# Weights, remainders, activations and 4 KB tiles at four offsets within 2048 bytes of a partition

## The chip, the cores and the metric

One core of a Trainium2 chip runs the kernel. The metric is the device time of one execution in microseconds. The kernel before was timed in three runs; one more execution was profiled, and all rows below come from that one.

## The reference, cut to what matters

Two transformer-like blocks are applied to one sequence of 256 tokens with 2048 features, all in float32.

```python
def reference(x, ...):
    x = first_block(x, ...)    # conv branch + forgetting attention, gated, then relu^2 MLP (d_ff 8192)
    return second_block(x, c, ...)   # ada-modulated: MoBA attention + SSM mixer, then conv FFN (5632 x 2)
```

Nearly all of the work is products of the 256 x 2048 activations with large weight matrices (`w_in`, `w_ff1`, `w_ff2`, `w_up`, `w_down` and smaller ones), 434 pieces of 1 MB in this kernel, and one vector-matrix product, `silu(c) @ w_ada`, of 96 MB.

## The kernel before, in words

**High and low parts.** The matmul engine takes `float32r` operands, which are rounded. To keep the accuracy of float32, each operand is kept as a high part (the value converted to `float32r`) and a remainder (the value less its high part), and three products are summed: high x high, high x remainder, remainder x high.

**Pieces.** A weight matrix is packed on the host into pieces of 128 partitions x 2048 columns (8 KB per partition). `piece` (line 102) takes one: the SP queue loads it to `wraw` (line 62), the scalar engine copies it to `wH` with a conversion (line 122), the vector engine subtracts `wH` from `wraw` and writes the remainder `wL` (line 123). `wraw`, `wH` and `wL` have three buffers each in the pool `wp`. A piece is converted at once or, where it is waited for, in four parts of 512 columns.

```python
raw = wp.tile([P, 2048], F32, tag="wraw", ...)                      # 106
h = wp.tile([P, 2048], FR, tag="wH", ...)                           # 108
l = wp.tile([P, 2048], FR, tag="wL", ...)                           # 109
...
A.activation(h[:, sl], raw[:, sl], AF.Copy)                         # 122
ins = V.tensor_tensor(l[:, sl], raw[:, sl], h[:, sl].bitcast(F32), op=OP.subtract)   # 123
```

**Two kinds of product.** `bblock` (line 139) and `wide` (line 186) give a transposed result: the piece is the stationary operand, the activations move. One piece is 16 matmuls with 128 x 128 blocks of `wH` over 512 columns (the high part and the remainder of an activation chunk side by side) and 16 with blocks of `wL` over 256 columns (the high part alone). These are the projections `cc`, `cv`, `cb`, `gc`, `ga`, `q`, `k`, `z`, `co`, `ao`, `ff1` and `up`. `ablock` (line 229) and `down_last` (line 955) give a result with tokens on the partitions: the activations are stationary, the piece moves. One piece is 24 matmuls of 512 columns: `uh` with `wH`, `ul` with `wH`, `uh` with `wL`. These are `v`, `mix`, `wo`, `ff2` and `dn`. Every matmul has a weight load of its own, and all go through `mm` (line 128).

```python
def hi(k, n):                                                       # 153, in bblock
    mm(ps[:, n, :], h[:, k, n * P:(n + 1) * P], xs[k][2], ...)
def lo(k, n):                                                       # 156
    last_mm[0] = mm(ps[:, n, S:2 * S], l[:, k, n * P:(n + 1) * P], xs[k][0], ...)
```

**Where the tiles lie.** Pools are laid behind one another in a partition, in the order in which they are opened: `cp` (small constants, line 42), `wp` (line 43), `sb` (line 44), `tp` (line 45). `wp` holds nine tiles of 8 KB. `sb` holds tiles of 16 KB (`xs`: the residual stream; `a16`: `cyc`, `atc`, `wHL`, `xx`), of 8 KB (`r8`: broadcast rows; `act`: four chunks of activations, made by `act_chunk` on line 64, each with four times 1 KB of high part and 1 KB of remainder in turn) and of 4 KB (`q4`: seven buffers for results and for `uh`, `ul`). `tp` holds short tiles of 2 KB and less.

**What sets the order.** The order of the instructions on each engine is planned when the kernel is built, from modelled times; loads on the SP queue are kept in program order. The piece's buffers set how far loads run ahead. `ada` (line 94) puts one 1 MB piece of `w_ada` into the same `wraw` buffers now and then and lets the vector engine multiply and sum it (line 99). At the start, `h1_tiles` loads `xT` in alternation with quarters of the first piece, a memset fills `mhalf` (line 86) and an activation on it (line 88) makes the scalar engine's table load early.

Of the kernel before, what the change touches and what calls it, by code (L numbers as in the profile page):

```python
# [7 lines left out]
F32 = mybir.dt.float32  # L8
FR = mybir.dt.float32r
# [4 lines left out]
P = 128  # L14
S = 256
# [20 lines left out]
def body(ctx: ExitStack, tc: tile.TileContext, x_d, xT_d, vec_d, con_d, rel_d, relc_d, gfin_d, c_d, fg_d,  # L36
# [3 lines left out]
    V, A, T, G = nc.vector, nc.scalar, nc.tensor, nc.gpsimd  # L40

    cp = ctx.enter_context(tc.tile_pool(name="cp", bufs=1))
    wp = ctx.enter_context(tc.tile_pool(name="wp", bufs=3))
    sb = ctx.enter_context(tc.tile_pool(name="sb", bufs=1))
    tp = ctx.enter_context(tc.tile_pool(name="tp", bufs=2))
    acc = ctx.enter_context(tc.tile_pool(name="acc", bufs=2, space=bass.MemoryType.PSUM))
# [8 lines left out]
    def a16(name, dt=FR):  # L55
        return sb.tile([P, 8, 2, S], dt, tag="a16", bufs=1, name=name)
# [4 lines left out]
    def load(dst, src):  # L61
        tc.keep_in_program_order(nc.sync.dma_start(dst, src))

    def act_chunk(name, i):
        hl = sb.tile([P, 4, 2, S], FR, tag="act", bufs=4, name=f"{name}A{i}")
        return hl[:, :, 0, :], hl[:, :, 1, :], hl

    xv = x_d.rearrange("(t p) d -> p t d", p=P)
    xT = sb.tile([P, KT, S], F32, tag="xs", name="xT")
    vec = cp.tile([P, NVEC], F32, name="vec")  # L70
# [20 lines left out]
    n_pc = [0]  # L91
    mod = cp.tile([P, 96], F32, name="mod")

    def ada():
        i = n_ada[0]
        n_ada[0] += 1
        w = wp.tile([P, D], F32, tag="wraw", name=f"wada{i}")
        load(w, wada_d[i])
        V.scalar_tensor_tensor(w, w, 1.0, c_bc, op0=OP.mult, op1=OP.mult,  # L99
                               accum_out=mod[:, i:i + 1])  # L100

    def piece(src, parts=1, feed=None, extra=None, nt=4, hold=None):
        n_pc[0] += 1
        if n_ada[0] < 96 and n_pc[0] > 18 and n_ada[0] < (n_pc[0] - 18) * 0.47:
            ada()
        raw = wp.tile([P, 2048], F32, tag="wraw", name=f"wraw{n_pc[0]}")
        if extra is None:
            h = wp.tile([P, 2048], FR, tag="wH", name=f"wH{n_pc[0]}")
            l = wp.tile([P, 2048], FR, tag="wL", name=f"wL{n_pc[0]}")
        else:  # L110
            hl = a16(f"wHL{n_pc[0]}").rearrange("p k b s -> p (k b s)")
            h, l = hl[:, 0:2048], hl[:, 2048:4096]
        if feed is None:
            load(raw, src)
        else:
            for i in range(4):
                feed(i)
                load(raw[:, i * 512:(i + 1) * 512], src[:, i * 512:(i + 1) * 512])
        w = 2048 // parts
        for i in range(parts):  # L120
            sl = slice(i * w, (i + 1) * w)
            A.activation(h[:, sl], raw[:, sl], AF.Copy)  # L122
            ins = V.tensor_tensor(l[:, sl], raw[:, sl], h[:, sl].bitcast(F32), op=OP.subtract)  # L123
            if hold is not None and i == 0:
                behind(ins, hold)
        return h.rearrange("p (k n) -> p k n", k=nt), l.rearrange("p (k n) -> p k n", k=nt)
# [4 lines left out]
    def behind(ins, prev):  # L131

        tc.add_manual_dep(ins.ins, prev.ins.name,
                          mybir.DependencyInfo(mybir.DependencyClass.NoSync, mybir.DependencyReason.DATA),
                          reason="behind")
# [3 lines left out]
    def bblock(W, nb, acts, name, dst, post=None, pre=None, nk=None, parts=1, feed=None, scale=None,  # L139
               mid=None):  # L140

        nk = nk or len(acts) // 8
        for hf in range(2):
            ps = acc.tile([P, 2, 512], F32, tag="acc", name=f"{name}_{hf}")
            for kg in range(nk):
                if pre is not None and hf == 0:
                    pre(kg)
                fd = feed if hf == 0 and kg == 0 else None
                h, l = piece(W[2 * nb + hf, kg], parts if hf == 0 or kg == nk - 1 else 1, fd, nt=8)
                last = kg == nk - 1  # L150
                xs = acts[8 * kg:8 * kg + 8]

                def hi(k, n):
                    mm(ps[:, n, :], h[:, k, n * P:(n + 1) * P], xs[k][2], kg == 0 and k == 0, False)

                def lo(k, n):
                    last_mm[0] = mm(ps[:, n, S:2 * S], l[:, k, n * P:(n + 1) * P], xs[k][0], False, last and k == 7)

                for ns in ((0,), (1,)) if last else (range(2),):
                    for f in (hi, lo):  # L160
                        for k in range(8):
                            for n in ns:
                                f(k, n)
            evict([ps[:, :, :]], dst, hf, scale, post)
            if mid is not None and hf == 0:
                mid()
        return dst
# [139 lines left out]
    def t_chunk(src, i, gname, acts):  # L307
        h, l, hl = act_chunk(gname, i)
        for b in range(2):
            ps = bank(f"tr{gname}{i}{b}")  # L310
            for k in range(2):
                kt = 4 * i + 2 * b + k
                for t in range(2):
                    T.transpose(ps[:, k * S + t * P:k * S + (t + 1) * P],
                                src[:, t, kt * P:(kt + 1) * P], ident)
            for k in range(2):
                kk = 2 * b + k
                kt = 4 * i + kk
                A.activation(h[:, kk, :], ps[:, k * S:(k + 1) * S], AF.Copy, scale=vc(gname, kt))
                V.scalar_tensor_tensor(l[:, kk, :], ps[:, k * S:(k + 1) * S], vc(gname, kt),  # L320
                                       h[:, kk, :].bitcast(F32), op0=OP.mult, op1=OP.subtract)
        acts.extend((h[:, k, :], l[:, k, :], hl[:, k]) for k in range(4))
# [6 lines left out]
    def norm2(src, r, av, bv, name):  # L329
        acts = []  # L330
        for i in range(4):
            h, l, hl = act_chunk(name, i)
            xs = []
            for t in range(2):
                xc = tp.tile([P, 512], F32, tag="t2k", bufs=4, name="xc")
                V.tensor_scalar(xc, src[i][:, t, :], r[:, t:t + 1], None,
                                op0=OP.mult)
                xs.append(xc)
            for b in range(2):
                ps = bank(f"tr{name}{i}{b}")  # L340
                for t in range(2):
                    for k in range(2):
                        kk = 2 * b + k
                        T.transpose(ps[:, k * S + t * P:k * S + (t + 1) * P],
                                    xs[t][:, kk * P:(kk + 1) * P], ident)
                for k in range(2):
                    kk = 2 * b + k
                    kt = 4 * i + kk
                    tt = tp.tile([P, S], F32, tag="t1k", bufs=6, name="nt")
                    A.activation(h[:, kk, :], ps[:, k * S:(k + 1) * S], AF.Identity,  # L350
                                 bias=bv[:, kt:kt + 1], scale=av[:, kt:kt + 1])
                    V.tensor_scalar(tt, ps[:, k * S:(k + 1) * S], av[:, kt:kt + 1],
                                    bv[:, kt:kt + 1], op0=OP.mult, op1=OP.add)
                    lt = V.tensor_tensor(l[:, kk, :], tt, h[:, kk, :].bitcast(F32), op=OP.subtract)
                    if kt == 7:
                        held[name] = lt
            acts.extend((h[:, k, :], l[:, k, :], hl[:, k]) for k in range(4))
        return acts
# [73 lines left out]
    def h1_tiles(h, l, hl, k0, k1):  # L432
        load(xT[:, k0:k1, :], xT_d[:, k0:k1, :])
        for kt in range(k0, k1):
# [6 lines left out]
    ccs = q4([P, 4, S], "ccs0")  # L441
    cvs = q4([P, 4, S], "cvs0")
    chunks = [act_chunk("h1", i) for i in range(4)]
    wide(win_d, (4, 5, 8, 9), h1, "cc0", lambda i: ((ccs, cvs)[i // 2], i % 2),
         feed=lambda q: h1_tiles(*chunks[q // 2], 2 * q, 2 * q + 2))
# [127 lines left out]
    for j in range(4):  # L573
        h, l, hl = act_chunk("mg", j)
# [530 lines left out]
```

## Time and profile before

| | |
|---|---|
| median of 3 runs | 2518.1 us (2514.66 to 2519.53) |
| profiled execution, its own time | 2515.24 us |
| its span, first to last instruction | 2513.5 us |
| matmul engine busy | 2481.0 us (99%) |
| vector engine busy | 1824.1 us (73%) |
| scalar engine busy | 1188.8 us (47%) |
| DMA engines, load queue | 61.4% of 16 engines, mean 228 GB/s |
| granted matmul clock, mean over the span | 0.996 |

A busy time is the union of an engine's instructions, and matmuls overlap by their pipeline: one takes 0.39 us from start to end, yet the next starts long before it ends. So the pace is read from the distance of two starts, or from a row that merges n matmuls: (its length less the length of one) / (n - 1).

### The profile page before, as it was taken

What the parts mean: (1) busy time and instruction counts of PE and PEld (TensorE: products, weight loads), DVE (VectorE), ACT (ScalarE), POOL (GpSimd) and SP (SyncE); (2) the same over time, 40 slices, a digit from 0 to 9 for tenths busy, and PEclk for the clock granted to TensorE, in tenths of its full rate; (3) what the DMA queues carried; (4) which work ended last, traced back from release to release, by engine and by line L of the source; (5) the groups of instructions that cost most, each with busy time, mean ns of one, the idle gap of its engine ahead of it and who ended that gap; (6) DMA issues with size and microseconds to landing.
All of it is one profiled execution on the core that took longest, in us unless ns stands there. A gap on an engine that the chain in (4) does not pass through costs nothing.

```text
span 2513.5 us, 31941 instructions
## 1 busy us (share of the span) xinstructions
PE 2481.0 (99%) x13202; PEld 2137.0 (85%) x13202; DVE 1824.1 (73%) x2011; ACT 1188.8 (47%) x1265; POOL 8.0 (0%) x16
## 2 busy tenths in 40 slices
PE   8999999999999999999998999999999999999998
PEld 7888888888888888888887888888888888888887
DVE  6787777787777777777756776575777777777768
ACT  6444444544544444444445544464544444444444
POOL 0000000000000000000000000000000000000000
PEclk9999999999999999999999999999999999999999
DMA  7677776678777777777656444455455555555553
GB/s 283 251 272 282 269 265 254 239 281 315 277 282 278 282 286 271 283 285 280 255 191 210 168 168 161 158 187 198 151 196 192 199 199 187 185 187 195 187 201 118
DMA packets 84977, 573.55 MB, mean 228 GB/s; under 512 B 9368, under 2 KB 10464, under 8 KB 16864
## 3 DMA queue, kind: packets, MB, share of 16 engines
q1 hardware_dynamic: 80352, 564.16, 61.4%
q10 hardware_dynamic: 4480, 7.36, 0.9%
q8 instruction: 103, 1.69, 0.3%
q14 instruction: 42, 0.34, 0.0%
HBM read 567.27 MB, written 4.21 MB: 227 GB/s over the span
## 4 chain that ended last, share of the span: by engine, by line
PE 96%; DVE 2%; ACT 1%; DMA 1%; issue 0%; POOL 0%; SPq 0%; ACTq 0%; POOLq 0%
PE ff L129 27%; PE up L129 20%; PE dn L129 9%; PE ga L129 4%; PE gc L129 4%; PE q L129 4%; PE k L129 4%; PE v L129 3%; PE wo L129 3%; PE mix L129 3%; PE cc L129 3%; PE z L129 2%; PE cb L129 2%; PE co L129 1%; PE ao L129 1%; PE xsc0p L129 1%
## 5 line engine op out<-in xcount | busy, mean ns | idle before, releaser
L123 DVE TENSOR_TENSOR wL<-wraw,wH 128x2048 fp32r<-128x2048 f32 (+1 forms) x511 | 998.5, 1963 | 532.8 <-ACT wH L122 524.1
L122 ACT ACTIVATE wH<-wraw 128x2048 fp32r<-128x2048 f32 (+1 forms) x511 | 837.8, 1653 | 1075.0 <-PE ff L129 359.6
L129 PE MATMUL up<-h4A,wH 128*128 128x512 f32 x1408 | 344.0, 391 | 0.0
L129 PEld LDWEIGHTS up<-h4A,wH 128*128 128x128 f32 x1408 | 256.6, 188 | 48.6 <-DVE up0r L179 0.2
L129 PE MATMUL ff<-g_mlpA,wH 128*128 128x512 f32 x1024 | 250.4, 392 | 0.0
L99 DVE SCALAR_TENSOR_TENSOR wada<-wada,c_bc 128x2048 f32<-128x2048 f32 x96 | 219.6, 2287 | 27.6 <-DMA wada<-in_wada 26.7
L129 PEld LDWEIGHTS ff<-g_mlpA,wH 128*128 128x128 f32 x1024 | 186.6, 188 | 35.7 <-issue 0.6
L129 PEld LDWEIGHTS up<-h4A,wL 128*128 128x128 f32 x1408 | 187.4, 192 | 10.3 <-ACT h4A L350 0.2
L129 PE MATMUL ff<-wH,uh 128*128 128x512 f32 x496 | 193.1, 390 | 0.0
L129 PE MATMUL ff<-wH,ul 128*128 128x512 f32 x496 | 192.9, 389 | 0.0
L129 PE MATMUL up<-h4A,wL 128*128 128x256 f32 x1408 | 191.3, 284 | 0.0
L129 PE MATMUL dn<-wH,vhl 128*128 128x512 f32 x640 | 158.3, 389 | 0.0
L129 PEld LDWEIGHTS ff<-g_mlpA,wL 128*128 128x128 f32 x1024 | 135.4, 191 | 7.4
L129 PEld LDWEIGHTS dn<-wH,vhl 128*128 128x128 f32 x640 | 119.5, 188 | 24.4
L129 PE MATMUL ff<-g_mlpA,wL 128*128 128x256 f32 x1024 | 137.9, 283 | 0.0
L129 PE MATMUL ff<-wL,uh 128*128 128x512 f32 x496 | 127.7, 389 | 0.0
L129 PEld LDWEIGHTS ff<-wH,uh 128*128 128x128 f32 x496 | 93.2, 188 | 19.4 <-issue 0.2
L129 PEld LDWEIGHTS ff<-wH,ul 128*128 128x128 f32 x496 | 93.1, 188 | 19.4 <-issue 0.2
L129 PEld LDWEIGHTS ff<-wL,uh 128*128 128x128 f32 x496 | 93.1, 188 | 19.4
L129 PE MATMUL dn<-wL,vhl 128*128 128x512 f32 x320 | 85.5, 389 | 0.0
L129 PEld LDWEIGHTS dn<-wL,vhl 128*128 128x128 f32 x320 | 60.1, 188 | 12.5
L129 PE MATMUL ga<-h1A,wH 128*128 128x512 f32 x256 | 64.6, 396 | 1.3 <-DVE aos L179 1.3
(559 smaller groups left out, 3172.2 us busy)
## 6 DMA issues: line engine op xcount, KB each, us to landing
wraw<-in_wff SPq DMA_DIRECT2D x128, 1024.0 KB, 4.8
wraw<-in_win SPq DMA_DIRECT2D x106, 1024.0 KB, 4.8
wada<-in_wada SPq DMA_DIRECT2D x96, 1024.0 KB, 4.8
wraw<-in_wup SPq DMA_DIRECT2D x88, 1024.0 KB, 4.8
wraw<-in_wdn SPq DMA_DIRECT2D x44, 1024.0 KB, 4.8
wraw<-in_wv SPq DMA_DIRECT2D x16, 1024.0 KB, 4.8
wraw<-in_wmix SPq DMA_DIRECT2D x16, 1024.0 KB, 4.9
wraw<-in_wout SPq DMA_DIRECT2D x16, 1024.0 KB, 4.8
```

The lines of the kernel that those rows point to most:

```text
L99: V.scalar_tensor_tensor(w, w, 1.0, c_bc, op0=OP.mult, op1=OP.mult, accum_out=mod[:, i:i + 1])
L122: A.activation(h[:, sl], raw[:, sl], AF.Copy)
L123: ins = V.tensor_tensor(l[:, sl], raw[:, sl], h[:, sl].bitcast(F32), op=OP.subtract)
L129: return T.matmul(o, l, r, start=first, stop=last, skip_group_check=True)
```

## The change

The remainder tiles `wL` get a pool of their own, `wlp`, and the `act` chunks one, `sa`; both are opened between `wp` and `sb`. In `wlp`, `sa` and `sb` a small tile named `gap`, of 32, 8 and 24 float32 (128, 32 and 96 bytes per partition), is allocated ahead of the others and filled by a memset on the vector engine. Nothing else differs.

```diff
     wp = ctx.enter_context(tc.tile_pool(name="wp", bufs=3))
+    wlp = ctx.enter_context(tc.tile_pool(name="wlp", bufs=3))
+    sa = ctx.enter_context(tc.tile_pool(name="sa", bufs=1))
     sb = ctx.enter_context(tc.tile_pool(name="sb", bufs=1))
...
     def act_chunk(name, i):
-        hl = sb.tile([P, 4, 2, S], FR, tag="act", bufs=4, name=f"{name}A{i}")
+        hl = sa.tile([P, 4, 2, S], FR, tag="act", bufs=4, name=f"{name}A{i}")
         return hl[:, :, 0, :], hl[:, :, 1, :], hl
 
+    for pool, w in ((wlp, 32), (sa, 8), (sb, 24)):
+        V.memset(pool.tile([P, w], F32, tag="gap", bufs=1, name="gap"), 0.0)
     xv = x_d.rearrange("(t p) d -> p t d", p=P)
...
             h = wp.tile([P, 2048], FR, tag="wH", name=f"wH{n_pc[0]}")
-            l = wp.tile([P, 2048], FR, tag="wL", name=f"wL{n_pc[0]}")
+            l = wlp.tile([P, 2048], FR, tag="wL", name=f"wL{n_pc[0]}")
```

## Rows read from the trace of the kernel before

**Rows 1.** The page: span, and busy time of each engine.
```profile
span 2513.5 us, 31941 instructions
PE 2481.0 (99%) x13202; PEld 2137.0 (85%) x13202; DVE 1824.1 (73%) x2011; ACT 1188.8 (47%) x1265; POOL 8.0 (0%) x16
```

**Rows 2.** Busy time by stage; behind the engines granted clock, DMA share, GB/s.
```profile
0.00:6.20 6.20, 0.00 (x0) 0.00 (x1) 0.96 (x4) 3.53 (x6) 0.20 (x4) 1.00 0.62 169
6.20:1378.00 1371.80, 1362.85 (x7190) 1171.83 (x7190) 1013.17 (x940) 632.68 (x628) 1.95 (x3) 1.00 0.73 269
1378.00:1390.00 12.00, 10.38 (x64) 9.41 (x65) 10.71 (x32) 5.89 (x12) 1.21 (x2) 0.76 0.06 22
1390.00:1764.00 374.00, 370.86 (x2046) 319.06 (x2044) 246.55 (x374) 188.18 (x241) 3.01 (x4) 1.00 0.50 177
1764.00:1783.00 19.00, 15.68 (x89) 14.23 (x90) 17.66 (x43) 9.82 (x21) 0.55 (x1) 0.82 0.16 58
1783.00:2490.00 707.00, 706.95 (x3755) 610.99 (x3754) 520.12 (x597) 340.34 (x342) 0.00 (x0) 1.00 0.53 189
2490.00:2513.50 23.50, 14.23 (x63) 11.45 (x61) 14.89 (x28) 8.36 (x20) 1.08 (x2) 0.86 0.25 89
```

**Rows 3.** The chain that ended last: start, length, engine, result, number of matmuls.
```profile
1995.55 44.59 PE up L129 x256
2040.14 21.79 PE dn L129 x96
```

**Rows 4.** Timeline: start, length, engine, line, operation, tiles, count; idle time before.
```profile
1101.47 0.39 PE L129 MATMUL ff<-wH,uh 128*128 128x512 f32 x1
1101.70 0.39 PE L129 MATMUL ff<-wH,ul 128*128 128x512 f32 x1
1101.92 0.39 PE L129 MATMUL ff<-wH,uh 128*128 128x512 f32 x1
...
1103.24 2.29 DVE L99 SCALAR_TENSOR_TENSOR wada<-wada,c_bc 128x2048 f32<-128x2048 f32 x1 [1.85 <-DMA wada<-in_wada]
1103.29 1.07 PE L129 MATMUL ff<-wL,uh 128*128 128x512 f32 x4
1103.48 1.92 ACT L122 ACTIVATE wH<-wraw 128x2048 fp32r<-128x2048 f32 x1 [4.42 <-PE ff L129]
1104.19 0.39 PE L129 MATMUL ff<-wH,uh 128*128 128x512 f32 x1
1104.42 0.39 PE L129 MATMUL ff<-wH,ul 128*128 128x512 f32 x1
...
2006.52 3.82 PE L129 MATMUL up<-h4A,wH 128*128 128x512 f32 x16
2010.17 2.08 PE L129 MATMUL up<-h4A,wL 128*128 128x256 f32 x16
2012.08 1.09 PE L129 MATMUL up<-h4A,wH 128*128 128x512 f32 x4
```

**Rows 5.** Timeline of the first microseconds: vector and scalar engine.
```profile
0.81 0.06 DVE L86 MEMSET mhalf<- 128x2 f32 x1 [0.81 <-PEq L1092]
2.48 0.20 ACT L88 ACTIVATE warm<-mhalf 128x2 f32<-128x2 f32 x1
4.11 0.63 ACT L452 ACTIVATE junk<-xT 128x512 f32<-128x512 f32 x1 [1.43 <-DMA xT<-in_xT]
5.17 0.89 DVE L437 SCALAR_TENSOR_TENSOR h1A<-xT,vec,h1A 128x256 fp32r<-128x256 f32 x2 [4.30 <-ACT h1A L436]
```

**Rows 6.** Groups by line and shape: count, busy us, mean ns; then line 123's shortest/median/longest.
```profile
L123 DVE TENSOR_TENSOR wL<-wraw,wH 128x2048 fp32r<-128x2048 f32 x407 | 932.1, 2290 | 513.3 <-ACT wH L122 509.5 <-PE k L129 2.2 <-PE q L129 0.8
L99 DVE SCALAR_TENSOR_TENSOR wada<-wada,c_bc 128x2048 f32<-128x2048 f32 x96 | 219.6, 2287 | 27.6 <-DMA wada<-in_wada 26.7
L784 DVE TENSOR_SCALAR lah<-con,adt 128x128 fp32r<-128x128 f32 x32 | 6.8, 280 | 0.0
L122 ACT ACTIVATE wH<-wraw 128x2048 fp32r<-128x2048 f32 x407 | 780.1, 1917 | 1039.8 <-PE ff L129 359.3 <-PE up L129 143.3 <-PE dn L129 95.4
L123 DVE TENSOR_TENSOR wL<-wraw,wH x511: 678/2291/2295, 6.2 to 2488.5; 128x2048 fp32r<-128x2048 f32 x137, 128x512 fp32r<-128x512 f32 x34
L123 DVE TENSOR_TENSOR wHL<-wraw,wHL x4: 679/681/682, 2481.9 to 2484.9; 128x512 fp32r<-128x512 f32 x4
```

**Rows 7.** The stretch at granted clock 0.50: busy times, and the matmuls in it.
```profile
1770.40:1772.90 2.50, 2.50 (x13) 2.50 (x12) 2.50 (x8) 1.72 (x4) 0.00 (x0) 0.50 0.00 0
L129 PE MATMUL up<-h4A,wL 128*128 128x256 f32 x12 | 2.8, 417 | 0.0
1770.42 2.80 PE L129 MATMUL up<-h4A,wL 128*128 128x256 f32 x12
```

**Rows 8.** Timeline of transposes, and their shortest/median/longest with their weight loads.
```profile
656.78 0.60 PE L314 MATMUL trg_mlp<-con,x 128*128 128x128 f32 x4
L314 PEld LDWEIGHTS trg_mlp<-con,x x32: 138/140/143, 597.8 to 666.7; 128*128 128x128 f32 x32
L314 PE MATMUL trg_mlp<-con,x x32: 270/272/273, 598.1 to 666.8; 128*128 128x128 f32 x32
```

## The prediction

> **What bounds the kernel now.** I read the page's busy table first: the matmul engine is busy 2481.0 us of a span of 2513.5, the vector engine 73%, the scalar engine 47% [rows 1]. A table by stage then shows where the 32.5 us are that it is not busy: 6.2 at the start, 9.0 in the long first half, 1.6 and 3.3 at the two norms, 3.1 between them, 9.3 at the end, and in 707 us of the last feed-forward stage 0.05 [rows 2]. In those 707 us nothing but the pace of the matmuls sets the time. The chain of waits says the same: one `up` block is one uninterrupted piece of 256 matmuls, the `down` call behind it one of 96 [rows 3].
>
> So the next view is the time from one matmul's start to the next's. In an `ff2` piece (`ablock`, line 229; 512 columns each) starts follow at 0.23 us, and eight of them from 1101.47 to 1103.29 make 1.82 / 8 = 227 ns [rows 4]. In `up` (`bblock`, line 139) the 16 with low weights, 256 columns each, start at 2010.17 and the next group at 2012.08: 1.91 / 16 = 119.5 ns; the 16 before them, 512 columns, take 3.65 / 16 = 228 ns [rows 4]. [...]
>
> **The change part by part.** *What moves.* In `wp` every tile is 8 KB, and in `sb` every size is a multiple of 4 KB, so before the change all weights, activations and 4 KB tiles begin at one and the same place within 2048 bytes; only `cp` and `tp` differ. Behind the change `wL` begins 128 bytes further on than `wH` and `wraw`, the `act` tiles 128 + 32 = 160 further, and all that stays in `sb` 128 + 32 + 96 = 256 further. A matmul with `wH` and `act` thus reads two streams 160 bytes apart, `wL` and `act` 32 bytes, `wH` and `uh`/`ul` 256, `wL` and `uh` 128. No matmul, conversion or load is added, removed or put on another queue; slots and their counts per tag stay.
>
> *What is added: three memsets.* The only memset of the vector engine in the trace took 0.06 us for 2 columns at 0.81 us; 32 columns can't be more than the 0.28 us that line 784 takes for 128 [rows 5, 6]. Three are 0.18 to 0.84 us, on the vector engine ahead of the memset of `mhalf`. Behind that queue stands the `warm` activation, which ran at 2.48 after a table load that waited for no memset; the scalar engine then sat idle for 1.43 us until the first load landed, and the vector engine until 5.17 [rows 5]. The memsets hide in that idle time: zero. Without that cover they would cost at most 0.84 us, 0.03%.
>
> *What the stationary and the moving read do to each other.* The trace has no pair of these tiles at different offsets, so I bound the effect. [...] Between them I take zero, for three reasons that the rows give:
>
> 1. Within a tile the weights already stand at four distances from the moving operand. `bblock` loads columns `k`, `n` at 1024 k + 512 n bytes, `ablock` loads halves of `uh` at 1024 k + 512 t, while the moving operand begins at a multiple of 2048. The eight single starts of rows 4 run through `k`, those behind 1104.19 are the same with the other `t`, and all step by 0.22 or 0.23. A distance of a multiple of 512 bytes changes nothing.
> [...]
> [...]
>
> Nor do the other engines' reads and writes show in the pace: the four matmuls from 1103.29 ran while both a conversion and a `wada` product ran, and need (1.07 - 0.39) / 3 = 227 ns; the eight before them ran with both engines idle, but for the last 0.05 us [rows 4]. [...]
>
> *The conversions.* `wraw` and `wH` keep their start, so the scalar copy reads and writes where it did, 1917 ns; the subtraction reads where it did and only writes 128 bytes further, 2290 ns, with 2295 as the longest [rows 6]. The `wada` product, also 2048 columns from two streams, writes onto the first of them and takes 2287 [rows 6]: 3 ns is what the place of the written stream is worth there, 407 x 3 = 1.2 us, either way, on an engine that is idle 27% of the time. Zero on the path; uncovered, 1.2 us.
>
> *Sum.* 0 + 0 + 0. The profiled execution's own time is 2515.2 us, its span 2513.5; it lies 2.9 us under the median of 2518.1, within the runs' spread of 2514.7 to 2519.5. I predict the median, **2518 us**.
>
> **The rivals.**
>
> [...]
>
> [...]
>
> *Another order of the instructions.* The order on each engine comes from a plan over modelled times, and three instructions more at its start, and tiles in four pools, can tip a tie. Slower: a piece that arrives late makes the matmul engine wait for a copy and a subtraction, 1.92 + 2.29 = 4.2 us; three such are 12.6: **2531 us**. Faster: the stages up to the second norm hold 9.0 + 1.6 + 3.1 + 3.3 = 17 us of idle matmul time [rows 2]; half of that is 8.5: **2509.5 us**. Against: the plan meets the first loads with the memsets long done.
>
> *The change doesn't do what it says.* If the pools' starts are rounded up to more than the gaps, the offsets stay equal and only the memsets are left: **2518 us**.
>
> **How the numbers follow.** A measurement of this kernel can tell about 0.2%, 5 us. Chances: no effect 0.58; pools rounded 0.04; order slower 0.11, order faster 0.07; reads parted 0.13; new collision 0.07. Same is 0.58 + 0.04 = 0.62, faster 0.07 + 0.13 = 0.20, slower 0.11 + 0.07 = 0.18. The range leaves out the two collision cases (0.20) and reaches to the two cases of order with the 1 us of noise either way: 2508 to 2532.
>
> **What would show it.** Right: 512-column starts 227 ns apart and 256-column starts 120 in the same stretches, `up` blocks near 44.6 us, `down` calls near 21.8, the same numbers of instructions but for three memsets before 2 us, first matmul at 6.2 us. Wrong by parting: a step under 220 ns in `ff2` or `up`. Wrong by a new collision: `up`'s low matmuls over 120 ns while the high ones stay. Wrong by order: equal steps but other idle time than 32.5 us in the table by stage.

## The result, and the profile after

The changed kernel takes 2537.7 us (2537.3 to 2538.4, four runs) against 2516.4 for the kernel before on the same chip: a ratio of 1.0082, 95% interval 1.0069 to 1.0094. It is 21 us slower, where no change was forecast, and lies outside the range of 2508 to 2532.

The page of the changed kernel shows the same work, three memsets more, and a matmul engine as full as before: 2535.5 - 2503.2 = 32.3 us of the span without a matmul, 32.5 before [rows 1].

```profile
span 2535.5 us, 31944 instructions
PE 2503.2 (99%) x13202; PEld 2129.8 (84%) x13202; DVE 1825.9 (72%) x2014; ACT 1189.0 (47%) x1265; POOL 8.0 (0%) x16
```

The start is what the prediction had: the memsets merge into 0.14 us, `warm` runs at 2.48 as in [rows 5]. Timeline of the changed kernel, vector and scalar engine:

```profile
0.81 0.14 DVE L71 MEMSET gap<- 128x32 f32 x3 [0.81 <-PEq L1096]
0.90 0.06 DVE L90 MEMSET mhalf<- 128x2 f32 x1
2.48 0.20 ACT L92 ACTIVATE warm<-mhalf 128x2 f32<-128x2 f32 x1
```

The conversions kept their pace, 2291 and 1917 ns (2290 and 1917 in [rows 6]). Groups by line and shape of the changed kernel, where the lines quoted stand four further down than in the kernel before:

```profile
L127 DVE TENSOR_TENSOR wL<-wraw,wH 128x2048 fp32r<-128x2048 f32 x407 | 932.4, 2291 | 536.2 <-ACT wH L126 532.1 <-PE k L133 2.1 <-PE q L133 0.8
L126 ACT ACTIVATE wH<-wraw 128x2048 fp32r<-128x2048 f32 x407 | 780.4, 1917 | 1062.1 <-PE ff L133 371.4 <-PE up L133 150.3 <-PE dn L133 97.7
```

The time is in the pace of the matmuls, and there alone. The pieces of the chain of waits that answer to [rows 3], with the longest of all, which took 631.97 us before:

```profile
690.24 637.53 PE ff L133 x3216
...
2080.44 44.88 PE up L133 x256
2125.32 22.02 PE dn L133 x96
```

An `up` block has grown from 44.59 to 44.88 and a `down` call from 21.79 to 22.02, with the same number of matmuls. The timeline says that two things happened in `up`, with opposite signs:

```profile
2024.61 3.89 PE L133 MATMUL up<-h4A,wH 128*128 128x512 f32 x16
2028.34 2.03 PE L133 MATMUL up<-h4A,wL 128*128 128x256 f32 x16
2030.21 2.03 PE L133 MATMUL up<-h4A,wH 128*128 128x512 f32 x8
```

Sixteen matmuls with high weights take 2028.34 - 2024.61 = 3.73 us, 233 ns each, against 228 in [rows 4]; sixteen with low weights take 1.87 us, 117 ns each, against 119.5. Done for the whole trace (the gap from each matmul's start to the next one's, where it is under 300 ns, by the tiles that the matmul reads):

| stationary, moving | count | distance before, after (bytes, modulo 256) | mean ns before, after | sum |
|---|---|---|---|---|
| `wH`, `act` | 4167 | 0, 96 | 227.6, 231.7 | +16.9 us |
| `wL`, `act` | 4185 | 0, 224 | 120.1, 118.3 | -7.7 |
| `wH`, `cyc` or `atc` | 256 | 0, 0 | 230.1, 230.2 | 0.0 |
| `wL`, `cyc` or `atc` | 252 | 0, 128 | 119.0, 120.3 | +0.3 |
| `act`, `wH` | 758 | 0, 160 | 227.1, 233.8 | +5.1 |
| `act`, `wL` | 379 | 0, 32 | 226.8, 232.5 | +2.2 |
| `uh` or `ul`, `wH` | 1711 | 0, 0 | 227.0, 228.2 | +2.2 |
| `uh`, `wL` | 855 | 0, 128 | 226.7, 231.6 | +4.2 |

The distance is where the weight block (the stationary operand) starts, less where the moving one does, in bytes within a partition. `wH` with `act` includes 64 matmuls of 256 columns in the two small projections; the other 4103, of 512 columns, go from 229.3 to 233.5 ns. The sum is +23.2 us, with -1.2 us in all other gaps: 22.0, the difference of the spans. The theory after this table: **the distance between the two reads of a matmul sets its pace, in a pattern that repeats every 256 bytes**, and distance 0 was a good place for 512 columns. One row doesn't fit it as it stands: `uh` or `ul` with `wH` slowed by 2.2 us at an unchanged distance of 0. There only the first three matmuls behind a run with `wL` are slower, 232, 233 and 231 ns; from the fourth on they take 226.7 as before. Rivals: the order of the instructions, the place of single tiles, the other engines.

### The profile page after: what moved, and what is told of

The parts are those of the page before. It is cut to its first block, busy times and chain, and to the rows that moved or that the text cites. A ratio compares the mean times of both kernels' runs of the same rounds, so it can differ in the third digit from the quotient of the medians.

```text
span 2535.5 us, 31944 instructions
## 1 busy us (share of the span) xinstructions
PE 2503.2 (99%) x13202; PEld 2129.8 (84%) x13202; DVE 1825.9 (72%) x2014; ACT 1189.0 (47%) x1265; POOL 8.0 (0%) x16
## 4 chain that ended last, share of the span: by engine, by line
PE 97%; DVE 2%; ACT 1%; DMA 0%; issue 0%; POOL 0%; ACTq 0%; POOLq 0%; DVEq 0%
PE ff L133 27%; PE up L133 20%; PE dn L133 9%; PE ga L133 4%; PE gc L133 4%; PE v L133 4%; PE q L133 4%; PE wo L133 4%; PE mix L133 4%; PE k L133 4%; PE cc L133 3%; PE z L133 2%; PE cb L133 2%; PE co L133 1%; PE ao L133 1%; PE bcsp L133 1%
## 5 line engine op out<-in xcount | busy, mean ns | idle before, releaser
L133 PE MATMUL up<-h4A,wH 128*128 128x512 f32 x1408 | 350.1, 396 | 0.1
L133 PEld LDWEIGHTS dn<-wH,vhl 128*128 128x128 f32 x640 | 119.5, 188 | 26.3
```

The costliest lines, as they stand in the source:

```text
L133: return T.matmul(o, l, r, start=first, stop=last, skip_group_check=True)
```

## The experiments

**1. All distances, matmuls alone.** A kernel that only loads and converts `x` and multiplies blocks of it, 16 matmuls to a group, one group to a distance. The moving block stays, the weight block moves.

```python
for i in range(16):
    o = 1024 + byte // 4 + 512 * (i % 2)
    T.matmul(ps[:, 0:cols], B[:, o:o + P], B[:, 0:cols], ...)
```

> Matmuls alone: no scalar, vector or DMA work beside them, and none of the reference's computation. Groups of 16 matmuls, in which a weight block and a moving block start at a chosen distance: 0 to 2016 bytes in steps of 32 (512 columns, then 256), then 0 to 252 in steps of 4. Theory 1 (the start of the weight block less that of the moving block sets the pace, in a pattern that repeats every 256 bytes): 227 ns at 0, 256, 512 and so on, up to 231 to 235 at 128 and 160, and for 256 columns about 118 at the small distances against 120 at 0. Theory 2 (the pace depends on where a tile starts, or on what the scalar and vector engines do, and not on the distance): 227 and 120 ns in all groups.

Timeline, one row for a group; the start of the next group is its end. `haa` to `hai` are 512 columns at 0, 32, ... 256 bytes:

```profile
21.95 3.80 PE L38 MATMUL haa<-B 128*128 128x512 f32 x16
25.58 3.89 PE L38 MATMUL hab<-B 128*128 128x512 f32 x16
29.31 3.90 PE L38 MATMUL hac<-B 128*128 128x512 f32 x16
33.04 3.90 PE L38 MATMUL had<-B 128*128 128x512 f32 x16
36.78 3.88 PE L38 MATMUL hae<-B 128*128 128x512 f32 x16
40.50 3.90 PE L38 MATMUL haf<-B 128*128 128x512 f32 x16
44.23 3.84 PE L38 MATMUL hag<-B 128*128 128x512 f32 x16
47.91 3.89 PE L38 MATMUL hah<-B 128*128 128x512 f32 x16
51.63 3.80 PE L38 MATMUL hai<-B 128*128 128x512 f32 x16
```

At 0 a group takes 25.58 - 21.95 = 3.63 us, 227 ns a matmul; at 96 (`had`) 3.74, 234 ns; at 256 all is as at 0, and so on through all eight periods of 256 up to 2016. Of the last 12 gaps of each group the means are 226.7 at every multiple of 256, 228.8 to 228.9 at 192, 232.5 to 234.6 elsewhere. In steps of 4 bytes the pattern is irregular: 226.7 again at 120, 144, 156, 204, 228 and 252, 236.7 at 212. For 256 columns 120.0 at 0, between 113.3 and 122.1 elsewhere. So moving the weight block alone does it, with no other engine at work, and of the distances tried for 512 columns **none is better than 0**. Whether the distance counts or the weight block's own place, this scan can't tell; experiment 4 does. One warning stood in this run: at 224 bytes the group in the scan by 32 runs at 116.7 ns and the one in the scan by 4 at 120.0. The pace also depends on what ran before.

**2. Pools and memsets, no distances.** This diff and those of 3 and 4 are against the changed kernel.

```diff
-    for pool, w in ((wlp, 32), (sa, 8), (sb, 24)):
-        V.memset(pool.tile([P, w], F32, tag="gap", bufs=1, name="gap"), 0.0)
+    for w in (32, 8, 24):
+        V.memset(cp.tile([P, w], F32, name=f"gap{w}"), 0.0)
```

> The three pools and the three memsets stay, but the gaps are small tiles in the constants' pool, so every weight, remainder, activation and 4 KB tile begins at one place within 2048 bytes again. Theory 1 (distances): back to 2516 within 5 us, 512-column starts 227 ns apart, 256-column starts 120. Rival (pools or memsets change the order of the instructions): 2538 within 5 us, with the idle time between matmuls as in the changed kernel.

Measured: 2516.7 us, ratio 1.0004 (0.9994 to 1.0014). The pools, the memsets and a common shift of all tiles by 256 bytes cost nothing; `up` and `down` are back at 44.59 and 21.79 in the chain of waits:

```profile
1994.65 44.59 PE up L133 x256
2039.23 21.79 PE dn L133 x96
```

**3. Four offsets within 2048 bytes that are multiples of 256.**

```diff
-    for pool, w in ((wlp, 32), (sa, 8), (sb, 24)):
+    for pool, w in ((wlp, 64), (sa, 64), (sb, 64)):
```

> The changed kernel with all three gaps at 256 bytes: four different offsets within 2048 bytes as well (0, 256, 512, 768), but every distance is a multiple of 256. Theory 1a (the pattern repeats every 256 bytes, as in the scan of distances): 2516 within 5 us, 227 and 120 ns. Rival 1b (any difference within 2048 bytes costs): 2537 or more.

Measured: 2516.9 us, ratio 1.0003 (0.9993 to 1.0013). Four different offsets within 2048 bytes are harmless as such; what counts is the distance modulo 256. The chain of waits:

```profile
1992.80 44.59 PE up L133 x256
2037.38 21.79 PE dn L133 x96
```

**4. Only the activation chunks moved.**

```diff
-    for pool, w in ((wlp, 32), (sa, 8), (sb, 24)):
+    for pool, w in ((sa, 40), (sb, 24)):
```

> Only the activation chunks move, by 160 bytes; remainders and 4 KB tiles stay at the high weights' place (distances of 0 modulo 256). From the scan: high weights less act = -160 = 96 modulo 256, 234.6 ns instead of 226.7; remainders less act the same 96, 117.2 instead of 120.0; v, mix and wo, where act is stationary, 160, 233.3. Counted with the changes that the changed kernel shows in the same groups: high weights +18 us, low weights about -11, v, mix and wo +8: 2531 within 6. If the chunks' place is not what costs, 2516.

Measured: 2537.4 us, ratio 1.0082 (1.0066 to 1.0098), just over the 2531 within 6. An `up` block is slow, a `down` call, which doesn't read the `act` chunks, is not:

```profile
2013.20 45.02 PE up L133 x256
2058.22 21.81 PE dn L133 x96
```

By the table's groups: `wH` with `act` +19.0 us (18 expected), `act` with `wH` and `wL` +4.7 and +2.5 (8 expected), the groups with `uh` and `ul` +0.3, as they should be at distance 0; but `wL` with `act` -4.7 and not -11. The groups of equal matmuls told the sign for the low weights and not the size.

This run also shows that the distance counts, and not the place of either tile by itself. The scan moved the weight block, this kernel moves the other operand of `wH` with `act`; yet the gaps go in the scan's own round of seven at 96 bytes (232, 237, 238, 231, 234, 235, 233 ns), in 113 of 114 runs of 16. `act` with `wL` is the sharper case, because the stationary `act` lies 160 bytes further on here and in the changed kernel. With `wL` in its old place, distance 160, every third gap is 237 or 238 ns in all 33 runs of 8, as in the scan at 160. With `wL` 128 further on, distance 32 in the changed kernel, no gap of 33 such runs is over 235, as in the scan at 32.

**5. Only the remainders moved, by 52 bytes.** One of the first scan's two best places for 256 columns. This diff and that of 7 are against the kernel before.

```diff
-            l = wp.tile([P, 2048], FR, tag="wL", ...)
+            l = wp.tile([P, 2048 + 64], FR, tag="wL", ...)[:, 13:13 + 2048]
```

> Only the remainders move, by 52 bytes within a wider tile of the same pool; all else as in the kernel before. From the scan: 256-column matmuls with weights 52 bytes further than the moving operand start every 113.3 ns instead of 120.0, and 512-column matmuls at the opposite distance (-52 = 204 modulo 256) at 226.7 as before. 4,416 matmuls x 6.7 = 29 us: 2487, within 10. If the scan's groups of 16 equal matmuls do not carry over to runs of 8 and 16 between others: 2516.

Measured: 2532.0 us, ratio 1.0060 (1.0044 to 1.0075): slower, neither of the two expected. The low matmuls of `up` fell into a round of 120, 118 and 122 ns instead of 113.3, and a `down` call, where the remainders move, became slower. Chain of waits, and timeline of a `down` call:

```profile
2005.44 44.68 PE up L129 x256
2050.12 22.23 PE dn L129 x96
```

```profile
1999.72 2.00 PE L129 MATMUL dn<-wH,vhl 128*128 128x512 f32 x8
2001.56 1.10 PE L129 MATMUL dn<-wL,vhl 128*128 128x512 f32 x4
2002.50 2.00 PE L129 MATMUL dn<-wH,vhl 128*128 128x512 f32 x8
```

Four matmuls with `wL` take 2002.50 - 2001.56 = 0.94 us, 235 ns each, at a distance (-52 = 204) where sixteen equal ones had run at 226.7. By the table's groups 11.3 us lie with the moving `wL` and 4.9 with the high matmuls of the same pieces, whose distance is still 0: the first five behind a run with `wL` take 233, 235, 228, 232 and 231 ns. The low weights of `act` gave back 1.2 us, not 29. The distances matter as before, but the scan was the wrong instrument for their price: a pace belongs to a distance and to the run that leads into it.

**6. A scan with the kernel's own runs.** Matmuls alone again, but in the kernel's sequence: `bblock`'s 16 high (distance 0) and 16 low (0 to 252 bytes), the same in runs of 8 as for a last piece, and `ablock`'s 24; each twice, the second one counts.

> Matmuls alone, none of the reference's computation: 16 high and 16 low matmuls in turn as in bblock (high weights at distance 0, low weights at 0 to 252 bytes in steps of 4), the same in runs of 8, and ablock's 24. Theory 1: the runs of low weights are shortest near 52, 64, 76 and 88 bytes (113.3 to 114 ns each), 120 at 0; ablock is shortest where the opposite distance is one of 0, 120, 144, 156, 204, 228 and 252. If the pace is a matter of equal repeated addresses alone, no place is under 118.

A piece of `bblock` at 0, 52, 76 and 204 bytes takes 5567, 5606, 5480 and 5627 ns, in runs of 8 5587, 5560, 5520 and 5653; `ablock`'s piece takes 5440 at 0 and more at every other place (5540 at 52, 5507 at 76). Timeline at 0 (`baa`) and 76 bytes (`bat`), second repetition, with the start of the group behind:

```profile
26.51 3.82 PE L51 MATMUL baa<-act,wH 128*128 128x512 f32 x16
30.17 2.08 PE L54 MATMUL baa<-act,wL 128*128 128x256 f32 x16
32.08 3.83 PE L51 MATMUL bab<-act,wH 128*128 128x512 f32 x16
...
237.53 3.81 PE L51 MATMUL bat<-act,wH 128*128 128x512 f32 x16
241.19 1.99 PE L54 MATMUL bat<-act,wL 128*128 128x256 f32 x16
243.01 3.82 PE L51 MATMUL bau<-act,wH 128*128 128x512 f32 x16
```

The low half falls from 32.08 - 30.17 = 1.91 us to 243.01 - 241.19 = 1.82. Of the four places named in the expectation 76 and 88 are short; in runs of 16, 64 is only 27 ns under the piece at 0, and 52 is 39 over it. For `ablock` only the place 0 came true: the six others expected take 5473 to 5554 ns. And this scan accounts, after the fact, for experiment 5: (39 - 27) / 2 ns x 276 pieces of `bblock` and `wide` + 100 ns x 156 pieces of `ablock` and `down_last` (both counted from the loops) = 17 us, 2533 against the 2532 measured.

**7 and 8. The scan as a forecast, both ways.** The remainders move only in pieces in which they are weights.

```diff
-            l = wp.tile([P, 2048], FR, tag="wL", ...)
+            l = wp.tile([P, 2048 + 64], FR, tag="wL", ...)
+            l = l[:, 19:19 + 2048] if nt == 8 else l[:, 0:2048]
```

(19 floats are 76 bytes; the other kernel has 51, 204 bytes.)

> As the kernel before, but in pieces whose remainders are weights (bblock, wide) the remainders begin 76 bytes further on; where they move (ablock, down_last) they stay at distance 0. The scan of runs gave 5480 ns for 16 high and 16 low matmuls at 76 bytes and 5520 in runs of 8, against 5567 and 5587 at 0: 77 ns a piece on average, 276 pieces, 21 us. Theory 1: 2495 within 5. If the scan does not carry over: 2516.

Measured: **2495.8 us, ratio 0.9920 (0.9906 to 0.9934)**, 20 us under the kernel before on the same chip and 42 under the changed one, as forecast. `wL` with `act` went from 120.1 to 115.5 ns, -19.2 us, all other groups within 1.4 us. Timeline and chain of waits:

```profile
2000.87 3.81 PE L130 MATMUL up<-h4A,wH 128*128 128x512 f32 x16
2004.52 1.99 PE L130 MATMUL up<-h4A,wL 128*128 128x256 f32 x16
2006.35 2.00 PE L130 MATMUL up<-h4A,wH 128*128 128x512 f32 x8
```
```profile
2044.82 43.98 PE up L130 x256
2088.79 21.79 PE dn L130 x96
```

The sixteen low ones take 1.83 us, 114 ns each; an `up` block 43.98 us instead of 44.59, a `down` call the 21.79 of before.

> The same edit at 204 bytes, the slowest place of the scan of runs: 5627 and 5653 ns a piece, 63 more than at 0 on average, 276 pieces, 17 us. Theory 1: 2533 within 5. If the scan does not carry over, or any shift helps: 2516 or less.

Measured: 2530.5 us, ratio 1.0057 (1.0043 to 1.0071), forecast 2533 within 5. `wL` with `act` 123.3 ns, +13.1 us; an `up` block takes 45.08:

```profile
2007.43 45.08 PE up L130 x256
```

## Why the prediction was wrong

**What bounds the kernel: right.** The matmuls' pace sets the time; 32.3 us without a matmul against 32.5, and gaps of under 300 ns account for +23.2 of the +22.0 us, all others for -1.2.

**The memsets, the order, the conversions: right at zero.** Experiment 2 has the pools, the memsets and their order but no distance, and measures 1.0004; the subtraction that writes further on takes 2291 ns in the changed kernel, 2290 before. The two rivals of another order and of rounded pools are out by the same run.

**The step that failed** is "Between them I take zero". The term put at zero measured +22 us. The cost does depend on the shift: 226.7 ns at 0 and 234.6 at 96 bytes, matmuls alone. No run shows the two ends that the zero lies between, nor what the columns alone take at granted clock 1.00; in their place the runs show means from 226.7 to 236.7 ns for 512 columns and from 113.3 to 122.1 for 256, by the distance. The scan shows rhythms: at 160 bytes the gaps repeat 231, 238, 231, at 0 they stay at 227. What holds a matmul up is not shown: the weight loads of `mix` with `wH` take 188 ns in the mean at 0 bytes in the kernel before and at 160 in the changed one.

**Reason 1 was true and too weak.** Distances of multiples of 512 bytes are equal (steps of 0.22 or 0.23 us in [rows 4]); so are those of 256 (experiment 3: 44.59 and 21.79 us, as before). The rows of before held no others between these tiles, so nothing in them spoke for or against the distances that the change made. That was the place to widen the range instead of choosing a middle.

**The stretch at granted clock 0.50 can't speak for a zero either.** There the gaps between low matmuls are 213 or 214 ns at distance 0 in the kernel before, the same at 224 bytes in the changed one and at 204 in experiment 8 (the merged row of [rows 7] gives 217, because its first gap is 360). Over the whole trace, at a mean granted clock of 0.996, `wL` with `act` takes 120.1, 118.3 and 123.3 ns at these distances. The price that hangs on distance there did not show at 0.50.

**The two collision cases (0.20 together).** Parting asked for a step under 220 ns in `ff2` or `up`. Distance 0 is the best of those tried for 512 columns, not the worst: no mean lies under 226.7 ns, the sixteen high matmuls of `up` went from 228 to 233, and the fastest kernel here gained 20 us. A new collision asked for low matmuls of `up` over 120 ns while the high ones stay. It had the sign of the total and the wrong pair: `wL` with `act` became 1.8 ns faster (-7.7 us), and most of the cost sits with `wH` and `act`, 160 bytes apart (96 in the table; +16.9 us). No group of the table changed by more than 7 ns.

## What to carry to other kernels

Where, as here, `float32r` matmuls follow one another, each with its own weight load, and set the time, the starts of the two operands within 256 bytes are worth trying as a tuning parameter (ratios of 0.9920 to 1.0082 here): measure the pace at a few distances, in the kernel's own sequence of runs and not in groups of equal matmuls, and give each kind of product its own distance. Tiles whose sizes are multiples of 256 bytes all lie at distance 0, which here was the best tried for 512 columns (226.7 ns) and not for 256 (120.0, against 113.3 at 52 bytes behind equal matmuls); a padding tile put between them cost 0.8% here, with nothing to see in the idle times. And when a trace shows only one value of what a change varies, neither "no effect" nor its size can be read from it.

## What the runs showed of the hardware that was not expected

- The pace repeats with a period of 256 bytes, with irregular steps of 4 bytes inside: 226.7 to 236.7 ns for 512 columns, 113.3 to 122.1 for 256.
- It depends on the run before: 256 columns at 52 bytes settle at 113.3 ns behind equal matmuls and at 118 to 122 behind 16 high ones, 224 bytes at 116.7 or 120.0. Even at distance 0 the first five 512-column matmuls behind a run of 256-column ones take 234, 236, 228, 232 and 231 ns in the second scan, the rest 227.
- At granted clock 0.50, 256 columns take 213 or 214 ns at 0, 204 and 224 bytes alike. The matmuls right behind the first one of each run take 426 or 427 ns for 512 columns, at 0 and at 96 bytes alike, though the granted clock on record there is 1.00. At granted clock 1.00 no distance tried brought the mean of 512 columns under 226.7 or of 256 under 113.3.
- What in the memory or in the array makes the pattern stays open. In the kernel's sequence the high weights of `bblock` were run at 0 and 96 bytes only; their other distances were tried in groups of equal matmuls.
